# Forming the right factors of a Strassen-like down projection on VectorE instead of GpSimd, one pair of units ahead

## The chip, the cores and the metric

The kernel runs on one core of a Trainium2 chip. The metric is the device time of one execution in microseconds, the median over several runs. Engines are named as the profile names them: PE is TensorE (PEld its weight loads), DVE is VectorE, ACT is ScalarE, POOL is GpSimd, SP is SyncE, whose queue issues nearly all DMAs.

## The reference

One layer of a decoder for a prompt of 1024 tokens and 64 sample tokens (8 sequences of 8), in float32. The change lies in the two SwiGLU blocks, so only their part is shown; between them stands a mixer (windowed attention beside a gated linear recurrence) that the change does not touch.

```python
D_MODEL = 1024; D_FF = 2816; SEQ = 1024; DEC_BATCH = DEC_SEQ = 8

def swiglu(x, w_gu, w_down):
    g, u = jnp.split(x @ w_gu, 2, axis=-1)
    return (jax.nn.silu(g) * u) @ w_down

x = x + 0.5 * rms_norm(swiglu(rms_norm(x, norm_ffn1_pre), ffn1_w_gu, ffn1_w_down), norm_ffn1_post)
x = x + mixer(x)                       # attention and recurrence
x = x + 0.5 * rms_norm(swiglu(rms_norm(x, norm_ffn2_pre), ffn2_w_gu, ffn2_w_down), norm_ffn2_post)
```

## The kernel before, in words

**Tokens and precision.** The 1088 rows are cut into three groups: group 0 (320 columns, with the sample tokens), and groups 1 and 2 (384 each). Every matrix operand is split into a high and a low half (`split`, L257: ScalarE casts at L258, VectorE subtracts at L259), and a product is three matmuls (`mm3`, L279 to L281).

**Up stage.** Groups 1 and 2 are multiplied together by a seven-product scheme of the Strassen kind (products named 1 to 7) instead of eight. A unit is one tile of 128 hidden columns of gate and up weight. There are 22 units, numbered u = 0 to 21, in an order in which two successive ones (2j and 2j+1) hold hidden tiles k and k+11: that is a pair, named by its odd number. `up` (L862) walks a list of steps. A step of kind "p" is one product of 12 matmuls: `product` issues it, `evict` takes the partial result out of PSUM (L763 to L776, on ScalarE and VectorE, with a GpSimd multiplication at L760). A step of kind "c" is a piece of the same hidden tile for group 0, where that has not been done before; in the first SwiGLU the first ten units have such steps. After each step `prepare` forms and splits the right factors needed up to four steps later: the raw weights come by L709, their differences are VectorE subtractions at L722, and the splits follow. `left` (L783) combines the outputs of a pair on GpSimd (L785 to L789) and stores them to a scratch tensor FA.

**Right factors of the down projection.** The down projection uses the same seven products, with the rows k and k+11 of the down weight as blocks. Four of its right factors are sums and differences of the blocks, formed per pair during the up stage and stored to a scratch tensor FB, from which the down stage reads them much later. `right_load` (L795) loads the rows of a pair into two tiles a and b (four DMAs of 256 KB at L800, on SP). `right_form` (L803) makes four subtractions of 128x512, L806, L807, L810 and L811, and stores the results (L809, L813). In the first SwiGLU two of the four are moreover split (`in_place`, L815) and the high half stored by L820. The tiles a and b come from a pool of 12 tiles named big, out of which come also six split factors that live through the stage and one output tile per unit.

**Order.** What stands here is the order in which instructions are written. When the program is built, a planner gives every engine an order of its own from estimated costs, readiness and free tiles; an instruction can so run well ahead of its written place on its engine, but each engine's and each DMA queue's order is then fixed, and an instruction that waits holds up those behind it. At the last unit of the first SwiGLU a hook (`begin_down`) starts the loads for the down projection of group 0: weights through L265, activations through L894.

In the version before, at product 1 of unit u the pair d is loaded and after product 7 of the same unit it is formed, with d as follows:

```python
d = 1 if u == 2 else u if u % 2 and u > 1 else 0
```

Of the kernel before, what the change touches and what calls it, by code (L numbers as in the profile page):

```python
# [14 lines left out]
ALU = mybir.AluOpType  # L15
# [30 lines left out]
def tile_step(ctx: ExitStack, tc: tile.TileContext, A: dict, O: list):  # L46
    nc = tc.nc
    V, S, G, PE = nc.vector, nc.scalar, nc.gpsimd, nc.tensor
# [51 lines left out]
    def tick():  # L100
        for name in list(streams):
            st = streams[name]
            st[2] += st[1]
            while st[2] >= 1.0:
                st[2] -= 1.0
                if next(st[0], "end") == "end":
                    del streams[name]
                    break
# [540 lines left out]
    def make_ffn(wgu, wdn, h, tag):  # L649
# [93 lines left out]
        def product(u, m):  # L743
            c, first, last = CHAIN[m]
            if first:
                chains[u, c] = mmbank()
            bk = chains[u, c][:, :384]
            w, (hi, lo) = right[u, m], f.SF[m]
            for k in range(4):
                mm3(bk, (w[:, 0, k], w[:, 1, k]), (hi[:, k], lo[:, k]), first and k == 0, last and k == 3, True)  # L750

        def evict(u, m):
            j = f.units[u][0]
            if m == 1:
                outs[u] = big()
            e = outs[u]
            bk = chains[u, CHAIN[m][0]][:, :384]

            def act(i):
                G.tensor_tensor(e[:, i], e[:, i], e[:, i + 1], op=ALU.mult)  # L760

            if m == 1:
                S.copy(e[:, 0], bk)  # L763
            elif m == 2:
                V.tensor_tensor(e[:, 0], bk, e[:, 0], op=ALU.add)
                S.activation(e[:, 0], e[:, 0], AF.Silu)
            elif m == 6:
                S.copy(e[:, 1], bk)
            elif m == 7:
                S.copy(e[:, 3], bk)  # L770
                V.tensor_tensor(e[:, 3], chains[u, "Y"][:, :384], e[:, 3], op=ALU.add)
            elif m == 4:
                S.activation(e[:, 2], bk, AF.Silu)  # L773
                act(2)
            elif m == 3:
                V.tensor_tensor(e[:, 1], bk, e[:, 1], op=ALU.add)  # L776
                act(0)
                if u % 2:
                    left(u)
# [15 lines left out]
        def right_load(u):  # L795
            k = f.units[u - 1][0]
            t1, t2_ = [big(F32, (P, 3, 512)) for _ in range(2)]
            for t, kk, o in ((t1, k, 0), (t2_, k + NK, 1)):
                for half in range(2):
                    nc.sync.dma_start(t[:, half ^ o], wrow(kk, half))  # L800
            downs[u] = t1, t2_

        def right_form(u):  # L803
            k = f.units[u - 1][0]
            a, b = downs.pop(u)
            G.tensor_tensor(a[:, 2], a[:, 1], a[:, 0], op=ALU.subtract)  # L806
            G.tensor_tensor(a[:, 1], b[:, 0], a[:, 1], op=ALU.subtract)  # L807
            in_place(7, k, a[:, 1])
            nc.sync.dma_start(FB[:, k, 0:2], a[:, 1:3])  # L809
            G.tensor_tensor(b[:, 2], b[:, 0], a[:, 2], op=ALU.subtract)  # L810
            G.tensor_tensor(b[:, 1], b[:, 1], b[:, 2], op=ALU.subtract)  # L811
            in_place(4, k, b[:, 1])
            nc.sync.dma_start(FB[:, k, 2:4], b[:, 1:3])  # L813

        def in_place(m, k, t):  # L815

            if m in halves:
                hi = pp.tile([P, 512], F32R, tag="t2", bufs=8, name=uid("fh"))
                split(hi, t.bitcast(F32R), t)
                nc.sync.dma_start(FH[:, k, halves[m]], hi.bitcast(F32))  # L820

        def piece(u, i):
            w = WIDTH[0]
            if i % 2 == 0:
                chains[u, "c", i // 2] = axbank("c0")
            bk = chains[u, "c", i // 2][:, :w]
            wt = right[u, (1, 2, 8, 3)[i]]
            for k in range(4):
                mm3(bk, (wt[:, 0, k], wt[:, 1, k]), hcol(h[0], 4 * (i % 2) + k, w), i % 2 == 0 and k == 0,
                    i % 2 == 1 and k == 3)  # L830
            if i == 1:
                chains[u, "g"] = gated0(f.units[u][0], bk)
            if i == 3:
                chains[u, "g"](bk)
# [22 lines left out]
        def prepare(i):  # L857
            while f.todo and f.todo[0][0] <= i + AHEAD:
                _, u, m = f.todo.pop(0)
                factor(u, m)  # L860

        def up(hooks={}):  # L862
            for i, (kind, u, m) in enumerate(f.steps):
                if kind == "p" and m == 1 and u in hooks:
                    hooks[u]()
                if kind == "p":
                    d = 1 if u == 2 else u if u % 2 and u > 1 else 0
                    if m == 1 and d:
                        right_load(d)
                    product(u, m)  # L870
                    evict(u, m)
                    if m == 7 and d:
                        right_form(d)
                else:
                    piece(u, m)
                prepare(i + 1)
                tick()
            for d in (raws, sums, right, chains, outs):
                d.clear()
# [149 lines left out]
        f.head = head  # L1029
        f.raw0 = raw0  # L1030
        f.loads0, f.up0, f.begin, f.up, f.begin_down, f.down = loads0, up0, begin, up, begin_down, down
        f.begin_pair, f.pair, f.gated0 = begin_pair, pair, both0
        return f
# [710 lines left out]
```

## Time and profile before

| | |
|---|---|
| median of 3 runs | 2006.42 us (2005.93 to 2008.47) |
| profiled execution, own time | 2007.32 us |
| its span, first to last instruction | 2005.5 us |
| granted TensorE clock | 0.999 |
| busy share PE, DVE, ACT, POOL | 99%, 71%, 47%, 28% |
| DMA, mean over the span | 185 GB/s |
| first up stage, about | 112 to 505 us |
| second up stage, about | 1434 to 1760 us |

The page's parts are read like this: busy time by engine, the span in slices, the DMA queues, the chain of work that ended last, and the costliest groups of instructions. A group's row gives line, engine, operation, tiles written and read, shape and count, then busy microseconds, mean nanoseconds of one, the idle time of the engine just before them, and what ended it. A row of waits gives who waited for whom, total microseconds, number of times and the longest.

### The profile page before, as it was taken

Reading aid. Unit: us, or ns where it says so; the run is one execution under the profiler, and the core shown is the slowest. Engines: PE = TensorE matmul, PEld = TensorE weight load, DVE = VectorE, ACT = ScalarE, POOL = GpSimd, SP = SyncE. Lnnn points to the kernel's source line nnn. Section 1 sums busy time; section 2 is a strip of 40 time slices with the busy share of each in tenths; the row PEclk is TensorE's granted clock in tenths of the full one; section 3 lists DMA queues with packets and bytes.
Section 4 is the critical chain, followed back from the end, with each engine's and each line's share of the span. In section 5 each row is a group of like instructions: output and inputs, shape, how many; then the busy total and the mean of one; then the engine's idle time right before and its main releaser. Section 6 shows DMA issues by size and latency. Waiting matters only on the chain.

```text
span 2005.5 us, 34728 instructions
## 1 busy us (share of the span) xinstructions
PE 1982.5 (99%) x13331; PEld 1854.6 (92%) x13331; DVE 1425.8 (71%) x2321; ACT 935.4 (47%) x1697; POOL 555.7 (28%) x516
## 2 busy tenths in 40 slices
PE   9999999999999999999999999999999999999998
PEld 8999999999998987897899898989999999999886
DVE  7676767887558656777668756857888888655666
ACT  5744333444445434445344544645544444444452
POOL 2013433655104101211112311220155565510201
PEclk9999999999999999999999999999999999999999
DMA  7735446566766756766434343527566555567874
GB/s 222 229 104 177 129 156 201 196 219 232 233 220 215 189 151 219 256 166 182 135 96 138 87 141 106 175 89 236 156 200 206 188 190 191 208 231 233 286 260 138
DMA packets 377319, 370.31 MB, mean 185 GB/s; under 512 B 40546, under 2 KB 294321, under 8 KB 377137
## 3 DMA queue, kind: packets, MB, share of 16 engines
q1 hardware_dynamic: 371169, 357.21, 56.3%
q10 hardware_dynamic: 5984, 10.88, 1.6%
q8 instruction: 105, 1.72, 0.3%
q14 instruction: 61, 0.50, 0.1%
HBM read 284.31 MB, written 84.71 MB: 184 GB/s over the span
## 4 chain that ended last, share of the span: by engine, by line
PE 87%; DVE 5%; DMA 4%; issue 2%; ACT 1%; POOL 1%; SPq 0%; DVEq 0%; ACTq 0%; POOLq 0%
PE mm L279 25%; PE mm L281 25%; PE mm L280 25%; DMA raw<-in_ffn_w_gu_dram 2%; PE pv L1212 1%; PE c L281 1%; PE c L279 1%; PE c L280 1%; PE sc L1171 1%; DMA ar<-act 1%; DVE t L722 1%; DVE w L259 1%; PE pT L1199 1%; PE lv L1244 1%; DVE big L259 1%
## 5 line engine op out<-in xcount | busy, mean ns | idle before, releaser
L279 PE MATMUL mm<-h,wsph 128*128 128x320 f32 (+1 forms) x1280 | 407.9, 320 | 1.1 <-ACT sg L675 1.1
L280 PE MATMUL mm<-h,wsph 128*128 128x320 f32 (+1 forms) x1280 | 405.4, 317 | 1.9 <-POOL h L259 1.9
L281 PE MATMUL mm<-h,wspl 128*128 128x320 f32 (+1 forms) x1280 | 404.2, 317 | 2.0 <-DVE wspl L259 2.0
L259 DVE TENSOR_TENSOR wspl<-raw,wsph 128x1024 fp32r<-128x1024 f32 x200 | 251.2, 1259 | 125.4 <-ACT wsph L258 124.7
L258 ACT CAST wsph<-raw 128x1024 fp32r<-128x1024 f32 x200 | 209.2, 1049 | 275.8 <-PE mm L280 198.9
L259 DVE TENSOR_TENSOR w<-raw,w 128x512 fp32r<-128x512 f32 (+1 forms) x218 | 228.9, 1054 | 82.6 <-ACT w L258 81.2
L258 ACT CAST w<-raw 128x512 fp32r<-128x512 f32 (+1 forms) x218 | 160.3, 739 | 213.1 <-PE mm L280 112.5
L281 PEld LDWEIGHTS mm<-h,wspl 128*128 128x128 f32 x1280 | 240.0, 188 | 5.7 <-issue 2.6
L279 PEld LDWEIGHTS mm<-h,wsph 128*128 128x128 f32 x1280 | 240.2, 188 | 5.3 <-issue 2.5
L280 PEld LDWEIGHTS mm<-h,wsph 128*128 128x128 f32 x1280 | 240.4, 188 | 4.2 <-POOL h L259 2.4
L279 PE MATMUL mm<-h,w 128*128 128x384 f32 (+1 forms) x720 | 240.3, 335 | 3.0 <-DVE big L776 1.5
L280 PE MATMUL mm<-h,w 128*128 128x384 f32 (+1 forms) x720 | 240.5, 334 | 0.0
L281 PE MATMUL mm<-h,w 128*128 128x384 f32 (+1 forms) x720 | 235.1, 334 | 0.0
L279 PE MATMUL mm<-w,h 128*128 128x512 f32 x462 | 181.0, 395 | 0.2 <-DVE big L971 0.2
L280 PE MATMUL mm<-w,h 128*128 128x512 f32 x462 | 181.1, 392 | 0.0
L760 POOL TENSOR_TENSOR big<-big 128x384 f32<-128x384 f32 x88 | 112.2, 1276 | 247.5 <-ACT big L773 144.6
L281 PE MATMUL mm<-w,h 128*128 128x512 f32 x462 | 179.7, 391 | 0.0
L279 PE MATMUL mm<-big,w 128*128 128x384 f32 x528 | 176.8, 335 | 2.7 <-ACT big L763 1.3
L280 PE MATMUL mm<-big,w 128*128 128x384 f32 x528 | 176.6, 334 | 0.0
L281 PE MATMUL mm<-big,w 128*128 128x384 f32 x528 | 176.4, 334 | 0.0
L259 DVE TENSOR_TENSOR w<-t,w 128x512 fp32r<-128x512 f32 x176 | 163.2, 935 | 14.6 <-ACT w L258 14.3
L279 PEld LDWEIGHTS mm<-h,w 128*128 128x128 f32 x720 | 135.0, 188 | 4.0 <-DVE big L776 1.8
(361 smaller groups left out, 3881.8 us busy)
## 6 DMA issues: line engine op xcount, KB each, us to landing
raw<-in_ffn_w_gu_dram SPq DMA_DIRECT2D x156, 512.0 KB
raw<-in_ffn_w_down_dram SPq DMA_DIRECT2D x74, 512.0 KB
raw<-in_w_in_dram SPq DMA_DIRECT2D x54, 512.0 KB
ar<-fa SPq DMA_DIRECT2D x70, 384.0 KB
big<-in_ffn_w_down_dram SPq DMA_DIRECT2D x88, 256.0 KB
fb<-big SPq DMA_DIRECT2D x44, 512.0 KB
fa<-big SPq DMA_DIRECT2D x22, 768.0 KB
raw<-fb SPq DMA_DIRECT2D x30, 512.0 KB
```

The lines of the kernel that those rows point to most:

```text
L258: S.copy(hi, src)
L259: (lo_eng or V).tensor_tensor(lo, src, hi.bitcast(F32), op=ALU.subtract)
L279: PE.matmul(out, a[0], b[0], start=first, stop=False, skip_group_check=resume)
L280: PE.matmul(out, a[0], b[1], start=False, stop=False, skip_group_check=resume)
L281: PE.matmul(out, a[1], b[0], start=False, stop=last, skip_group_check=resume)
L722: V.tensor_tensor(t, x, y, op=ALU.subtract)
L760: G.tensor_tensor(e[:, i], e[:, i], e[:, i + 1], op=ALU.mult)
L1171: PE.matmul(banks[g][:, i * 256:i * 256 + wk], zq[64 * g:64 * g + 64, 2 * pr + i, b * P:(b + 1) * P], kx[64 * g:64 * g + 64, k0:k0 + wk], ...
L1199: PE.transpose(bank[:, (i * nk + kb) * P:(i * nk + kb + 1) * P], pt[g][:, i, kb * P:(kb + 1) * P], ident)
L1212: PE.matmul(ob[:, hd * 64:hd * 64 + 64], pT[g][:, (i * nk + kb) * P:(i * nk + kb + 1) * P], vn[:, vb, g * 64:g * 64 + 64], start=kb == 0, ...
L1244: PE.matmul(b5[cs, n_, a], x[:, a, cs], y[:, a, cs], start=True, stop=True)
```

## The change

The four subtractions of `right_form` are issued on VectorE instead of GpSimd. The unit at which a pair is loaded and formed is changed too: pair 1 stays at unit 2 and pair 3 at unit 3, pair 5 moves from unit 5 to unit 4, and from unit 5 on each odd unit loads and forms the pair two units later, so that pair 7 is done at unit 5 and pair 21 at unit 19, and unit 21 does none. The number of loads, subtractions, splits and stores is the same.

```diff
         def right_form(u):
             k = f.units[u - 1][0]
             a, b = downs.pop(u)
-            G.tensor_tensor(a[:, 2], a[:, 1], a[:, 0], op=ALU.subtract)
-            G.tensor_tensor(a[:, 1], b[:, 0], a[:, 1], op=ALU.subtract)
+            V.tensor_tensor(a[:, 2], a[:, 1], a[:, 0], op=ALU.subtract)
+            V.tensor_tensor(a[:, 1], b[:, 0], a[:, 1], op=ALU.subtract)
             in_place(7, k, a[:, 1])
             nc.sync.dma_start(FB[:, k, 0:2], a[:, 1:3])
-            G.tensor_tensor(b[:, 2], b[:, 0], a[:, 2], op=ALU.subtract)
-            G.tensor_tensor(b[:, 1], b[:, 1], b[:, 2], op=ALU.subtract)
+            V.tensor_tensor(b[:, 2], b[:, 0], a[:, 2], op=ALU.subtract)
+            V.tensor_tensor(b[:, 1], b[:, 1], b[:, 2], op=ALU.subtract)
             in_place(4, k, b[:, 1])
             nc.sync.dma_start(FB[:, k, 2:4], b[:, 1:3])
@@ up
                 if kind == "p":
-                    d = 1 if u == 2 else u if u % 2 and u > 1 else 0
+                    d = {2: 1, 3: 3, 4: 5}.get(u, u + 2 if u % 2 and 4 < u < 20 else 0)
                     if m == 1 and d:
                         right_load(d)
                     product(u, m)
```

## The prediction

> **What bounds the kernel now.** I read the head of the page first, then TensorE's waits, then the stretches of the two stages that the change touches, then VectorE's groups there.
>
> ```profile
> span 2005.5 us, 34728 instructions
> PE 1982.5 (99%) x13331; PEld 1854.6 (92%) x13331; DVE 1425.8 (71%) x2321; ACT 935.4 (47%) x1697; POOL 555.7 (28%) x516
> ```
>
> TensorE (PE) is busy for 1982.5 of 2005.5 us. GpSimd (POOL), from which work is taken, is busy for 28% and cannot be the bound as such. What can be won is idle time of TensorE, 23 us in the whole span; what can be lost is time in which TensorE is made to wait. TensorE's waits, over the whole span:
>
> ```profile
> PE mm L281 <- DVE wspl L259: 2.0, 2, 1.3
> PE mm L279 <- DVE big L776: 1.5, 1, 1.5
> PE mm L279 <- ACT big L763: 1.3, 1, 1.3
> PE mm L279 <- ACT big L770: 0.8, 1, 0.8
> PE mm L279 <- ACT big L768: 0.8, 1, 0.8
> PE mm L279 <- DVE big L771: 0.7, 1, 0.7
> ```
>
> The columns are total, number of times, longest. L763, L768, L770, L771 and L776 are the evictions of the products in the up stages of the two SwiGLUs, where the changed code runs. The chain of waits (start, length, what) gives the places of four of the stops, each ended by the instruction named:
>
> ```profile
> 344.80 0.48 DVE big L771
> ...
> 350.02 0.47 ACT big L768
> ...
> 519.15 2.04 DVE wspl L259
> ...
> 1463.07 0.56 DVE big L776
> ```
>
> Two more, on L763 and L770, fall at 490 and 504 us; their rows come below. So in the up stages TensorE stood still at 345 (0.7 us), 350 (0.8), 490 (1.3) and 504 (0.8, the last unit of the first up stage) and at 1462 (1.5, the start of the second); the stop of 1.3 us at 520, for the low half of a weight, belongs to the first down stage. That is 6.4 us in all, and no more can be won here. The stages in stretches (columns: length, then busy time of PE, PEld, DVE, ACT, POOL with counts, granted clock, DMA share, GB/s):
>
> ```profile
> 112.00:345.00 233.00, 232.63 (x1411) 232.00 (x1409) 160.35 (x247) 90.82 (x174) 85.39 (x68) 1.00 0.48 155
> 345.00:490.00 145.00, 143.92 (x828) 143.61 (x829) 123.95 (x144) 62.35 (x122) 87.14 (x60) 1.00 0.63 216
> 1480.00:1740.00 260.00, 260.00 (x1502) 260.00 (x1501) 216.76 (x247) 108.69 (x210) 151.35 (x109) 1.00 0.58 195
> ```
>
> From 1480 to 1740 us TensorE does not pause once. VectorE (DVE) is the next engine: 216.76/260 = 83% there, 85% from 345 to 490. It is where the four subtractions go, so it decides.
>
> **The change part by part.** Per pair of units GpSimd loses four subtractions of 128x512 and VectorE gains them; there are 11 pairs in each SwiGLU, 88 subtractions in all.
>
> *The work moved.* GpSimd's four rows, for nine pairs, and VectorE's rows of the same size:
>
> ```profile
> L811 POOL TENSOR_TENSOR big<-big 128x512 f32<-128x512 f32 x9 | 15.7, 1741 | 0.0
> L810 POOL TENSOR_TENSOR big<-big,big 128x512 f32<-128x512 f32 x9 | 15.3, 1699 | 0.0
> L807 POOL TENSOR_TENSOR big<-big,big 128x512 f32<-128x512 f32 x9 | 13.9, 1546 | 3.0 <-DMA big<-in_ffn_w_down_dram 2.5
> L806 POOL TENSOR_TENSOR big<-big 128x512 f32<-128x512 f32 x9 | 13.1, 1453 | 37.5 <-DMA big<-in_ffn_w_down_dram 37.5
> ...
> L259 DVE TENSOR_TENSOR w<-t,w 128x512 fp32r<-128x512 f32 x72 | 70.0, 973 | 4.9 <-ACT w L258 4.9
> L259 DVE TENSOR_TENSOR w<-raw,w 128x512 fp32r<-128x512 f32 x50 | 57.1, 1142 | 0.6
> L722 DVE TENSOR_TENSOR t<-raw,t 128x512 f32<-128x512 f32 x34 | 36.4, 1070 | 0.6
> L722 DVE TENSOR_TENSOR t<-raw 128x512 f32<-128x512 f32 x17 | 18.6, 1092 | 0.6
> L722 DVE TENSOR_TENSOR t<-raw,raw 128x512 f32<-128x512 f32 x17 | 12.8, 753 | 16.3 <-DMA raw<-in_ffn_w_gu_dram 16.3
> ...
> L722 DVE TENSOR_TENSOR t<-raw,t x88: 673/691/1776, 115.9 to 1717.7; 128x512 f32<-128x512 f32 x88
> ```
>
> The last row, minimum/median/maximum in ns, is the key: an undisturbed VectorE subtraction takes 0.69 us, but many take up to 1.78. Four more cost 4 x 0.69 = 2.8 us of VectorE per pair. What comes back: VectorE's 190 instructions of this size in the stretch took 194.9 us where 190 x 0.69 = 131 would do, an excess of 64 us. POOL's four groups hold 13.1 + 13.9 + 15.3 + 15.7 = 58.0 of its 151.35 busy us there, so their share of the excess is 0.383 x 64 = 24 us, 2.7 us for each of nine pairs. That puts all excess down to GpSimd's activity; the bounds are nothing back and the whole excess, 64/9 = 7.1 us per pair, and I take 2.7, the share by busy time, because GpSimd's other instructions stay. VectorE's load thus hardly changes: +2.8 - 2.7.
>
> The Trainium skill ("SBUF — State Buffer", section "SBUF: two separate sides") says that VectorE with two SBUF inputs and GpSimd share one port pair as an exclusive lock, held for a whole instruction, and the loser blocks fully. The row that reaches 1.78 us agrees that one holds up the other, but at full blocking by four GpSimd instructions of at least 1.45 us VectorE would win back 5.8 us per pair, 3.0 net, where the excess shows 2.7 back; TensorE would still set the time, and only the first rival below would lose ground, whose deciding wait would rise by about 3 us.
>
> *Does VectorE have the room?* A pair lasts 29.1 us, and 29.1 x (1 - 0.834) = 4.8 us of it VectorE is idle in the second SwiGLU, 29.1 x (1 - 0.855) = 4.2 us in the first. The 29.1 us is the spacing of these rows, once per pair:
>
> ```profile
> 1558.59 1.46 POOL L785 TENSOR_TENSOR big<-big,big 128x384 f32<-128x384 f32 x1
> ...
> 1587.70 1.46 POOL L785 TENSOR_TENSOR big<-big,big 128x384 f32<-128x384 f32 x1
> ```
>
> So the cover holds; if it went, each us beyond it would cost one us per pair.
>
> *The wait added.* VectorE's first subtraction of a pair now waits for the rows of the down weight. Behind it in VectorE's queue stand the differences of L722, the low halves of the weight splits of L259 that TensorE needs, and the evictions L765, L771 and L776, which free PSUM banks; ScalarE's (ACT) L766 waits for L765. How long? Two rows of the same stretch are the bounds:
>
> ```profile
> POOL big L806 <- DMA big<-in_ffn_w_down_dram: 37.5, 9, 4.8
> ...
> DVE t L722 <- DMA raw<-in_ffn_w_gu_dram: 16.3, 16, 4.9
> ```
>
> GpSimd waited 4.2 us per pair (37.5/9), having nothing else to do; VectorE waits 1.0 us per unit (16.3/16) for transfers of the same queue. Nothing is the lower end; a gain is excluded, since VectorE did not wait for these rows before. I take 1.0, for the same engine under the same load, and 1.0 fits in 4.2.
>
> *The step ahead.* From unit 5 on, load and forming of a pair sit one pair earlier in the order; units 3, 4 and 5 each hold one, and the last pair hands over nothing: its forming moves from unit 21 to 19. With it move the four loads (L800), the stores L809 and L813 and, in the first SwiGLU, two splits with their stores L820, all past the raw loads of L709 on SP's queue. In mid stage this is the same set of instructions per 29.1 us, at the same place in a unit. GpSimd already ran ahead of its written place:
>
> ```profile
> L806 POOL TENSOR_TENSOR big<-big x22: 1283/1367/2255, 134.4 to 1727.2; 128x512 f32<-128x512 f32 x22
> ...
> L763 ACT COPY big<-mm x44: 472/479/482, 111.9 to 1740.7; 128x384 f32<-128x384 f32 x44
> ```
>
> The last forming began at 1727.2 us, before even the first product of its unit was evicted (1740.7), though it is written after the last. So the step ahead is worth nothing in the middle. At the end of the first up stage it is worth something:
>
> ```profile
> 483.84 0.62 ACT L258 CAST fh<-big 128x512 fp32r<-128x512 f32 x1 [2.78 <-POOL big L811]
> ...
> 484.87 0.42 SPq L820
> ...
> 485.38 4.91 DMA ar<-act
> ...
> 491.27 0.48 ACT big L763
> ...
> 504.17 0.72 ACT L258 CAST h<-ar 128x640 fp32r<-128x640 f32 x1 [1.44 <-DMA ar<-act]
> 504.80 0.47 ACT L770 COPY big<-mm 128x384 f32<-128x384 f32 x1
> ```
>
> The first and the last two rows are ScalarE's timeline, the others the chain of waits. ScalarE waits 2.78 us for the last forming, SP's queue holds the store L820 behind that, and behind it the load of the activations for the down stage; the transfer takes 4.9 us, its cast waits for it on ScalarE, and the eviction L763 stands behind the cast, so TensorE stops for 1.3 us. With the last pair formed at unit 19 the head of this chain is gone: the load can go 2.8 us earlier, more than the 1.3 needed. The next stop, 0.8 us at 504 (L770 behind a cast that waited 1.44 us for a later one of these loads), hangs on the same queue; I take it as gone too, with bounds of 0 and 0.8. Late next is the split at 520, whose chain has the final left combinations on GpSimd in it, which stay.
>
> *What stays.* The stops at 345 and 350 us are VectorE late by GpSimd's stretch, and VectorE gets as much work as it gets relief. The stop at 1462 lies where pairs 1 and 3 keep their place. I cost these at nothing, between -3.0 (all three gone) and +3.0 (each doubled).
>
> **Sum.** The profiled execution took 2007.32 us (span 2005.5 and 1.8 around it): 2007.32 - 1.3 - 0.8 = 2005.2. The median of the runs, 2006.42, is 0.9 lower, so I predict 2004.3 us.
>
> **The rivals.** *VectorE held up by late down weights (slower).* Of VectorE's idle 4.2 to 4.8 us per pair, about 1.8 are its own waits for raw weights (16.3 us in nine pairs), which stay; 2.7 are free. From a wait of 2.7 us per pair on, VectorE becomes the bound, and the rest goes to TensorE in some 15 steady pairs (ten in the second SwiGLU, five in the first). At 3.5 us, halfway to GpSimd's 4.2, that is 0.8 x 15 = 12 us: 2018 us. For it: in the row above GpSimd waited for these loads in all nine pairs. Against it: VectorE works down a longer queue and comes to them later. Chance 0.22.
>
> *All stops go (faster).* If VectorE is in effect relieved, the six stops vanish: 2006.4 - 6.4 = 2000.0 us. For it: three of them end with VectorE late. Against it: VectorE's sum is even, and the stop at 520 has other causes. Chance 0.15.
>
> *Nothing moves.* The order in which the program is built already ran the forming ahead, and another load of the same queue takes the place of the late one at 490: 2006.4. Chance 0.15.
>
> *Crowding at units 3 to 5.* Three units in a row then form a pair; VectorE's need there is (216.76/260 x 29.1 - 2.7)/2 + 2.8 = 13.6 of 14.55 us per unit. Should two more stops of the size of that at 1462 follow, it is 2004.3 + 3.0 = 2007.3. Chance 0.10.
>
> **How the numbers follow.** The forecast has 0.38. A measurement of this kernel tells about 0.2%, 4.0 us, from no change. Forecast, nothing and crowding lie within it: 0.63 the same; faster 0.15; slower 0.22. The likeliest case's own range is 2001.3 to 2007.3 (the three stops that stay, 3.0 either way). For 8 in 10 I go from 2000.5, which leaves out half of the faster case, up to 2013, which takes in the lower half of the slower one.
>
> **What would show it.** Right: no TensorE wait on L763 near 490; VectorE's mean for 128x512 nearer 0.85 than 1.05 us; its busy share in the second up stage within 2 points of 83%; no ScalarE wait on a POOL instruction for the fh cast; TensorE unbroken from 1480 to 1740. Wrong: VectorE idle for big<-in_ffn_w_down by over 2.7 us per pair, with TensorE waits on weight splits or L771 and L776 spread over the units; or the stop at 490 still there behind another load; or a time that moves by over 4 us with the up stages unchanged in length, from an order that was laid out otherwise elsewhere.

## The result, and the profile after

The changed kernel takes 1999.36 us (median of 6 runs, 1998.05 to 2002.7), the kernel before, run beside it, 2006.63 us (6 runs, 2004.81 to 2009.83). The ratio is 0.9965, 95% interval 0.9954 to 0.9975: faster by 7.3 us, where 2.1 were predicted, and just below the predicted range of 2000.5 to 2013. The profiled execution took 2000.92 us. Head of its page:

```profile
span 1999.2 us, 34712 instructions
...
PE 1981.9 (99%) x13331; PEld 1856.7 (93%) x13331; DVE 1416.2 (71%) x2409; ACT 937.8 (47%) x1697; POOL 423.6 (21%) x428
```

TensorE is as busy as before (1981.9 us against 1982.5); its idle time fell from 2005.5 - 1982.5 = 23.0 us to 17.3. TensorE's waits, first rows of the changed kernel that matter here (who for whom: total, times, longest):

```profile
PE tr L511 <- DVE big L493: 1.9, 1, 1.9
PE mm L281 <- DVE wspl L259: 1.7, 3, 1.3
...
PE mm L279 <- ACT big L770: 0.7, 1, 0.7
```

The first, at 65 us, lies ahead of the changed code and is missing in a second profile of the same kernel (run e0 below). So does the longest of the second row (1.3, before 60 us); its other two, 0.2 each, lie near 518 and 1766 us. The last row is the only stop of the up stages, at 1448 us. Of the six stops on which the prediction was built, four are gone, that at 520 is down to 0.2, and in place of the 1.5 us at 1462 stands the one at 1448, which ends with another eviction. The stretches, with the columns of the prediction:

```profile
345.00:490.00 145.00, 145.00 (x839) 145.00 (x838) 115.18 (x158) 65.43 (x126) 65.00 (x43) 1.00 0.61 209
1480.00:1740.00 260.00, 260.00 (x1502) 260.00 (x1502) 206.72 (x279) 111.38 (x215) 88.06 (x73) 1.00 0.57 195
```

VectorE has 36 more instructions to form nine pairs from 1480 to 1740 us, and still its busy time falls from 216.76 to 206.72 us. Its groups of this size there:

```profile
L259 DVE TENSOR_TENSOR w<-t,w 128x512 fp32r<-128x512 f32 x71 | 58.2, 821 | 2.4 <-ACT w L258 2.4
L259 DVE TENSOR_TENSOR w<-raw,w 128x512 fp32r<-128x512 f32 x48 | 38.7, 807 | 4.5 <-ACT w L258 4.0
L722 DVE TENSOR_TENSOR t<-raw,t 128x512 f32<-128x512 f32 x33 | 28.2, 854 | 0.6
L722 DVE TENSOR_TENSOR t<-raw,raw 128x512 f32<-128x512 f32 x16 | 12.8, 800 | 17.7 <-DMA raw<-in_ffn_w_gu_dram 17.7
L807 DVE TENSOR_TENSOR big<-big,big 128x512 f32<-128x512 f32 x9 | 11.9, 1320 | 0.6 <-DMA big<-in_ffn_w_down_dram 0.6
L810 DVE TENSOR_TENSOR big<-big,big 128x512 f32<-128x512 f32 x9 | 11.9, 1317 | 0.0
L722 DVE TENSOR_TENSOR t<-raw 128x512 f32<-128x512 f32 x16 | 11.1, 692 | 0.5
...
L811 DVE TENSOR_TENSOR big<-big 128x512 f32<-128x512 f32 x9 | 6.9, 771 | 0.0
L806 DVE TENSOR_TENSOR big<-big 128x512 f32<-128x512 f32 x9 | 6.9, 770 | 1.6 <-issue 1.0 <-DMA big<-in_ffn_w_down_dram 0.6
```

The splits' means drop from 0.97 and 1.14 us to 0.82 and 0.81. Two of the four new subtractions take 1.32 us, not 0.69; the reason is in the section on what the runs showed of the hardware.

### The profile page after: what moved, and what is told of

The parts are those of the page before. It is cut to its first block, busy times and chain, and to the rows that moved or that the text cites. A ratio compares the mean times of both kernels' runs of the same rounds, so it can differ in the third digit from the quotient of the medians.

```text
span 1999.2 us, 34712 instructions
## 1 busy us (share of the span) xinstructions
PE 1981.9 (99%) x13331; PEld 1856.7 (93%) x13331; DVE 1416.2 (71%) x2409; ACT 937.8 (47%) x1697; POOL 423.6 (21%) x428
## 4 chain that ended last, share of the span: by engine, by line
PE 93%; DMA 3%; DVE 2%; ACT 1%; issue 1%; SPq 0%; POOL 0%; DVEq 0%; ACTq 0%
PE mm L279 27%; PE mm L281 27%; PE mm L280 27%; PE pv L1212 1%; PE c L281 1%; PE c L279 1%; PE c L280 1%; PE sc L1171 1%; DMA raw<-in_ffn_w_gu_dram 1%; DMA ar<-act 1%; PE pT L1199 1%; PE tr L511 1%; PE lv L1244 1%; DMA ar<-fa 1%; DVE wspl L259 0%
## 5 line engine op out<-in xcount | busy, mean ns | idle before, releaser
L259 DVE TENSOR_TENSOR w<-raw,w 128x512 fp32r<-128x512 f32 (+1 forms) x218 | 202.7, 934 | 83.8 <-ACT w L258 82.4
L760 POOL TENSOR_TENSOR big<-big 128x384 f32<-128x384 f32 x88 | 121.3, 1378 | 638.2 <-ACT big L773 447.7
L259 DVE TENSOR_TENSOR w<-t,w 128x512 fp32r<-128x512 f32 x176 | 137.1, 788 | 10.3 <-ACT w L258 10.3
```

The lines of the kernel that those rows point to most:

```text
L259: (lo_eng or V).tensor_tensor(lo, src, hi.bitcast(F32), op=ALU.subtract)
```

## The experiments

The theories: *relief* (R: VectorE, no longer held up by GpSimd, serves TensorE sooner), *step ahead* (A: the last pair leaves the end of the stage), *another order elsewhere* (O: the planner lays out other instructions differently), *waiting* (W: casts, low halves and stores wait for GpSimd's slow results) and VectorE's *room*. All times are medians of 5 to 11 executions, each with its ratio to the kernel before in the same rounds and the 95% interval. e0 to e3 ran on one chip, e4 to e7, e8 to e10 and e11 with e12 on three others, so across these groups the ratios are compared, not the times.

**e0: the change once more.**

> The change itself once more, beside the others on one chip: 1999.4 us, ratio 0.9965 to before. Its profile is to show whether the extra stop of 1.9 us at 65 us (a transposition that waits for VectorE's L493), which its first profile has and that of before has not, belongs to the change or to the single execution: all theories expect that it comes and goes, since no pair is formed before 130 us.

1999.0 us, ratio 0.9958 (0.9946 to 0.9971): the gain is no accident of one run. Between 340 and 520 us a single TensorE wait, of 0.2 us, is left. At the start of the second up stage there is again one on L770, of 0.8 us.

**e1: the engine alone**, the old units.

```diff
-            G.tensor_tensor(a[:, 2], a[:, 1], a[:, 0], op=ALU.subtract)
+            V.tensor_tensor(a[:, 2], a[:, 1], a[:, 0], op=ALU.subtract)
 ... (the same for the other three)
```

> The four subtractions on VectorE, but every pair loaded and formed where it was before. Theory R (relief: VectorE is held up less, and the stops of TensorE that end with a late VectorE go): the stops at 345, 350 and 1463 us go, 3.0 us, and so does what a slow last forming costs at 490 to 521; VectorE's busy time in the second up stage falls by some 10 us per 260 as with the whole change; time 2000 to 2003 us against 2006.6 before. Theory A (ahead: what is gained comes from the last pair no longer formed at the end of the stage): the stops at 490 and 504 stay, and the time is 2005 to 2007. Theory O (the planner's other order elsewhere, in the mixer, brings some 2 us of it): a gain of up to 2 us may be missing or be larger, in stages in which no pair is formed.

2000.96 us, 0.9966 (0.9952 to 0.9979): most of the gain. The stops at 490 and 504 us are gone though the last pair is formed at unit 21 as before. One stop of 1.6 us remains near 350 (TensorE's waits), as long as the two at 345 and 350 were together, so at this place the engine alone wins nothing:

```profile
PE mm L279 <- ACT big L768: 1.6, 1, 1.6
```

**e2: the step ahead alone**, on GpSimd.

```diff
-                    d = 1 if u == 2 else u if u % 2 and u > 1 else 0
+                    d = {2: 1, 3: 3, 4: 5}.get(u, u + 2 if u % 2 and 4 < u < 20 else 0)
```

> The new units for load and forming, but the four subtractions on GpSimd as before. Theory R: GpSimd still holds VectorE up, the stops at 345, 350 and 1463 stay, only the end of the first up stage gains: 2003 to 2005. Theory A: the stops at 490, 504 and 521 go, 3.4 us, and most of the gain is there: 2000 to 2003. Theory O: as in the run of the engine alone, up to 2 us either way outside the up stages.

2005.19 us, 0.9989 (0.9981 to 0.9998). The end of the first up stage is clean here too (490, 504 and 521, stops of 3.4 us in the prediction's rows), but 345 and 350 stay and a new stop of 1.7 us comes at 1510, where units 3 to 5 each form a pair. The chain of waits that ends in it (start, length, what):

```profile
1501.03 5.62 DMA raw<-in_ffn_w_gu_dram
...
1506.74 0.69 DVE t L722
1507.43 1.44 DVE w L259
...
1510.18 0.56 DVE big L771
```

A raw weight lands at 1506.6, its difference and low half follow on VectorE, and the eviction L771 stands behind them; TensorE waits. This is the prediction's crowding, on GpSimd, and one stop instead of two. The times of the two parts add up (6.1 us for e1 and 1.9 for e2, beside 8.1 for e0 in the same rounds), but the stops do not: either part alone removes nearly all of those 3.4 us, and each leaves a stop that the whole change has not, 1.6 us at 350 in e1 and 1.7 at 1510 in e2. The sum of the times is thus in part a coincidence.

**e3, e4, e5: what GpSimd's forming costs, taken apart.** e3 is the change without the four subtractions; e4 adds four GpSimd subtractions per pair whose results nobody reads; e5 adds ten GpSimd memsets per pair instead.

```diff
-            V.tensor_tensor(a[:, 2], a[:, 1], a[:, 0], op=ALU.subtract)   # all four; stores take a[:, 0:2], b[:, 0:2]
+            G.tensor_tensor(t[:, 2], t[:, 0], t[:, 0], op=ALU.subtract)   # e4: twice for t in (a, b)
+            G.memset(t[:, 2], 0.0)                                        # e5: five times for t in (a, b)
```

> As the change, but the four subtractions are left out on either engine; the raw rows are stored in their place, so the products of the down projection are those of other factors. All loads, splits and stores stay. Theory R: VectorE's 88 subtractions lie in its idle time, so the time is that of the change within 1.5 us, about 1999; VectorE's other instructions of 128x512 are as long as with the change (about 0.8 us mean). If instead the subtractions on VectorE still cost TensorE something, this is 2 to 5 us faster than the change. Theory O: a difference of up to 2 us by order alone.

> As the run without forming (1998.45 us), and GpSimd makes four subtractions of 128x512 per pair whose result nobody reads (into parts of the tiles that are not stored). What is left out is as in that run: the real forming. VectorE's own work is that of the run without forming, and no engine waits for GpSimd's results. Theory R (GpSimd's activity alone lengthens VectorE's instructions, and that makes TensorE stop): VectorE's busy time from 1480 to 1740 us rises from 184 by 24 (2.7 us per pair, as the prediction had it) to 35 us (3.9, as the change gave back), stops of TensorE after 340 and near 1460 us come back, and the time is 2002 to 2005. Rival W (before, it was the waiting for GpSimd's slow results, by the casts on ScalarE and the stores on SP's queue): the time stays at 1998 to 1999.5.

> As the run before it, but GpSimd does ten memsets of 128x512 per pair instead of four subtractions: about as much busy time (10 x 0.53 against 4 x 1.3 to 1.7 us), and nothing read. If VectorE is held up by GpSimd's reads of its memory ports alone, VectorE's instructions of 128x512 stay as in the run without forming and the time is 1998 to 1999.5. If any GpSimd instruction holds it up, it is as in the run with the four subtractions, 2002 to 2005.

e3 1998.45 us, 0.9958 (0.9945 to 0.997); e4 1999.29, 0.9963 (0.995 to 0.9975); e5 1998.15, 0.9959 (0.9946 to 0.9971). The stretch from 1480 to 1740 us in e3, then in e4 with its added GpSimd group, then in e5 with its own:

```profile
1480.00:1740.00 260.00, 260.00 (x1502) 260.00 (x1501) 184.40 (x241) 111.06 (x213) 85.43 (x72) 1.00 0.57 190
```

```profile
1480.00:1740.00 260.00, 260.00 (x1502) 260.00 (x1501) 212.41 (x243) 110.88 (x213) 140.21 (x109) 1.00 0.57 196
```

```profile
L808 POOL TENSOR_TENSOR big<-big 128x512 f32<-128x512 f32 x36 | 48.5, 1355 | 32.7 <-DMA big<-in_ffn_w_down_dram 21.5 <-issue 10.4
```

```profile
1480.00:1740.00 260.00, 260.00 (x1502) 260.00 (x1501) 183.90 (x241) 111.06 (x214) 122.69 (x150) 1.00 0.57 190
```

```profile
L808 POOL MEMSET big<- 128x512 f32 x79 | 37.4, 527 | 0.6 <-DMA fb<-big 0.6
```

Three readings. The hold-up is real: with 48.5 us of GpSimd subtractions VectorE's nearly equal number of instructions takes 212.41 - 184.40 = 28.0 us longer, 3.1 us per pair. It comes from what the GpSimd instruction does, not from GpSimd being busy: 37.4 us of memsets cost VectorE nothing (183.90). And over a whole stretch it is nearly free in the time: e4 is 1.1 us slower than e5 on the same chip, by the ratios not told apart, and VectorE's 212 us out of 260 leaves TensorE unbroken. So VectorE's busy time by itself is not where the 7 us come from; e4's VectorE is nearly as busy as that of the kernel before, and the gain is still there. One reservation: e4's subtractions need less of the pair's rows and run in other moments. Ahead of the stop at 345 they end at 333.8 us, those of the kernel before at 336.3, so e4 doesn't repeat the hold-up at that place in full. At the same units real forming on GpSimd (e2) costs 2005.19 - 1998.45 = 6.7 us, on VectorE (e0) 0.6.

**e11, e12: waiting without hold-up.** The missing corner: GpSimd memsets write the tiles that are split and stored, so that the others wait for a GpSimd chain that doesn't hold VectorE up. e11 has the new units, e12 the old ones.

```diff
-            V.tensor_tensor(a[:, 2], ...) and the other three (e12: G.tensor_tensor)
+            for i in (1, 2, 1, 2, 1, 2):
+                G.memset(a[:, i], 0.0)        # then split and store as before; the same for b
```

> The change, its units kept, but the four subtractions of a pair are replaced by GpSimd memsets of 128x512 that write the tiles which are then split and stored, three over each, so that ScalarE's casts, VectorE's low halves and SP's stores wait for a GpSimd chain of about 6.3 us per pair (12 x 0.527) as they do when GpSimd forms (four times 1.36 to 1.74). The computation left out: the right factors are zeros. A memset does not hold VectorE up, so this is the corner that is missing: waiting without hold-up, beside hold-up without waiting (0.8 us dearer than neither), neither, and both (6.7 us dearer, the version with only the units moved). Theory of the waiting: the cost of forming on GpSimd is that its results come late and the casts and stores queue behind it: 2002 to 2005, with stops at 345 to 350 and near 1510. Rival, that it takes the hold-up and the waiting together: 1998 to 2000, no more than neither alone, VectorE near 184 us busy from 1480 to 1740.

> The same memsets in the kernel before, its units kept: waiting for a GpSimd chain without VectorE being held up, and the last pair formed at unit 21. The computation left out: the right factors are zeros. Theory of the waiting: the stops at the end of the first up stage (490, 504 and 520 us, 3.9 us) are there, for they hang on the chain GpSimd, cast, store, load of the activations, and those at 345 and 350 too: 2004 to 2007. Rival, hold-up and waiting together: the stops at 490 to 520 stay at half or less, those at 345 to 350 go: 1999 to 2002.

e11 1999.9 us, 0.9969 (0.9958 to 0.998); e12 1999.86, 0.9969 (0.9958 to 0.9979). The theory of the waiting by itself falls: both land in the rival's range, and in e12 no TensorE wait of over 0.2 us is left between 340 and 520 us, with the last pair at unit 21. The four corners, new units, in ratios: neither 0.9958 (e3), hold-up alone 0.9963 (e4), waiting alone 0.9969 (e11), both 0.9989 (e2). Against e3 that is 1.0 us for hold-up alone, 2.2 for waiting alone and 6.2 for both, each to about 3 us, so that both together cost more than the sum is likely but not clear of noise. TensorE's stops in and just behind the two up stages, from 340 us on, point the same way: 0.4 us in e3, 1.2 in e4, 1.2 in e11 and 4.0 in e2. How the two can strengthen each other can be read in GpSimd's timeline of the last pair, first the kernel before, then e12 (start, length):

```profile
475.47 1.30 POOL L806 TENSOR_TENSOR big<-big 128x512 f32<-128x512 f32 x1 [5.49 <-issue]
476.84 2.15 POOL L807 TENSOR_TENSOR big<-big,big 128x512 f32<-128x512 f32 x1
...
480.65 1.46 POOL L760 TENSOR_TENSOR big<-big 128x384 f32<-128x384 f32 x1
482.07 1.74 POOL L811 TENSOR_TENSOR big<-big 128x512 f32<-128x512 f32 x1
```

```profile
470.55 0.53 POOL L807 MEMSET big<- 128x512 f32 x1 [1.87 <-DMA big<-in_ffn_w_down_dram]
...
475.54 0.53 POOL L811 MEMSET big<- 128x512 f32 x1
```

Before, the chain begins at 475.5 and ends at 483.8, each step drawn out and an L760 in between; in e12 it ends at 476.1. By this reading hold-up makes the results late and VectorE late in using them. One reservation: a memset needs fewer of the pair's loads than a subtraction, so e12's chain also begins 5 us sooner; e11 and e12 bound waiting on a short chain, and waiting on a long chain without hold-up was not tried.

**e6: VectorE's room.** The change with four more VectorE subtractions per pair.

```diff
+            for t in (a, b):
+                for _ in range(2):
+                    V.tensor_tensor(t[:, 0], t[:, 0], t[:, 0], op=ALU.subtract)
```

> The change, and VectorE makes four more subtractions of 128x512 per pair, behind the real ones, on parts of the tiles that are no longer needed: eight instead of four. Theory R with room left: VectorE's busy time from 1480 to 1740 us rises from 207 by 9 x 2.8 = 25 to 232 to 240 of 260 us, still under the bound, and the time is within 2 us of the change, 1999 to 2001. If VectorE had no room, TensorE would stop in every pair: 28 us at most and over 2005.

2009.18 us, 1.0015 (1.0006 to 1.0024): the gain is lost and more, and neither expectation was met. Stretches of the columns above, and TensorE's longest wait:

```profile
345.00:490.00 145.00, 140.27 (x804) 139.00 (x803) 123.34 (x173) 61.91 (x120) 67.88 (x42) 1.00 0.63 207
1480.00:1740.00 260.00, 257.63 (x1482) 256.45 (x1481) 231.10 (x319) 106.40 (x208) 105.68 (x72) 1.00 0.57 193
```

```profile
PE mm L279 <- ACT big L768: 6.1, 4, 3.2
```

At 231 of 260 us (89%) TensorE loses 2.4 us in nine pairs, nearly all of it before 1520 us, where three units in a row form a pair, and 4.7 between 345 and 490. The room ends at such places first, not in the steady stretch. The added subtractions also stand ahead of the pair's last split and store, so e6 makes these late as well as VectorE busy.

**e7: `left` on VectorE too.** L785 to L789 moved as well.

```diff
-            G.tensor_tensor(e[:, 1], e[:, 2], e2[:, 2], op=ALU.add)
+            V.tensor_tensor(e[:, 1], e[:, 2], e2[:, 2], op=ALU.add)
 ... (the same for the other three)
```

> The change, and the four left combinations per pair (L785 to L789, 128x384) on VectorE too. Theory R: VectorE gains 4 x 0.55 = 2.2 us per pair and loses the time that these four hold it up, which the excess in the second up stage puts at 2.2 us per pair, so its sum is even; TensorE's stops in the up stages are already gone but for about 1 us, so it is the change within 1 us, 1998 to 2000. If it is faster by over 2 us, the relief acts elsewhere than in the stops; if slower by over 2, VectorE's order is too tight for the evictions.

1998.58 us, 0.9959 (0.9946 to 0.9971): the same as the change. Its VectorE is busy for 205.52 us from 1480 to 1740, 36 shorter subtractions more and 1.2 us less than the change:

```profile
1480.00:1740.00 260.00, 260.00 (x1502) 260.00 (x1501) 205.52 (x313) 110.35 (x212) 40.90 (x36) 1.00 0.57 192
```

**e8, e9, e10: a fourth tile for raw weights.** They test a loop: VectorE late, a raw tile free late, the next raw load issued late, the next evictions late. A fourth raw tile has room only if big gives one up; e10 is that control.

```diff
-NRAW = 3
+NRAW = 4                 # e8 on the kernel before, e9 on the change; not e10
-tag="big", bufs=12
+tag="big", bufs=11       # all three
```

> The kernel before (GpSimd forms, old units) with four tiles raw for weights on their way in instead of three, and to make room eleven tiles big instead of twelve. Engine and order of the forming are untouched. Theory of the loop: GpSimd's subtractions hold VectorE up, and that costs time only where a late VectorE frees a tile raw late, so that the next raw weights are issued and land late and the evictions behind them are late too. With a fourth tile the load is issued sooner, and the stops of the kernel before at 345, 350 and 1463 us go (3.0 us) with VectorE's busy time from 1480 to 1740 still near 217 us; those at 490 to 521 us stay: 2004, and stops of the weight splits elsewhere may change too. Rival, hold-up itself: VectorE has not enough time for splits and evictions together at these places, whatever the number of tiles: 345, 350 and 1463 stay, 2007. If a tile big less hurts, the control with eleven shows it.

> The change with four tiles raw and eleven tiles big. Theory of the loop: the change has little left of these stops (0.7 us at 1448), so a fourth tile brings at most 1 us: 1998 to 1999.5. Rival, that the change left half of the loop in place, hidden in places without a stop over 0.2 us: over 2 us faster, 1997 or less.

> Control: the kernel before with eleven tiles big and three raw. The pairs' down weights and six split factors share these tiles. Theory: a free tile more or less shifts the loads of down weights by at most one unit and nothing waits for them: 2007, within 2 us of the kernel before, with the stops at 345, 350 and 1463. Rival: the loads come later, GpSimd's forming too, and the end of the first up stage is worse: 2009 or more.

e8 2019.0 us, 1.006 (1.0048 to 1.0073); e9 2011.43, 1.002 (1.0011 to 1.0029); e10 2017.17, 1.0047 (1.0033 to 1.006). The control missed: a big tile less costs 10 us, in the mixer and not in the up stages (below), so these times say little and the stretches must do. The stretch from 335 to 360 us in the kernel before, with the load L709 of SP's timeline that matters there; the stretch in e10; and both again in e8:

```profile
335.00:360.00 25.00, 23.55 (x134) 22.91 (x133) 22.24 (x30) 10.09 (x21) 11.42 (x9) 1.00 0.70 236
```

```profile
341.38 0.38 SPq L709 DMA_DIRECT2D raw<-in_ffn_w_gu_dram  x1
```

```profile
335.00:360.00 25.00, 23.67 (x135) 22.88 (x134) 22.01 (x30) 10.22 (x22) 10.23 (x8) 1.00 0.72 244
```

```profile
335.00:360.00 25.00, 25.00 (x147) 25.00 (x146) 22.71 (x28) 12.12 (x25) 12.99 (x10) 1.00 0.68 234
```

```profile
338.05 1.80 SPq L709 DMA_DIRECT2D raw<-in_ffn_w_gu_dram  x2
```

With the fourth tile the loads go out at 338 instead of 341.4 and the stops at 345 and 350 vanish, with VectorE no less busy than before. That half of the theory stands: the two stops are a matter of when the raw tile comes free. (In e0 the same load goes at 337.7, with three tiles.) The other half fails: at the start of the second up stage TensorE stops for 2.5 us in e8, more than the 1.5 of the kernel before, and e8 has a new stop of 1.1 us on L763 between 240 and 280 us.

## Why the prediction was wrong, by its own steps

**Bounds and the ceiling.** Reading TensorE's idle time as all there is to win was right in kind: the span fell by 6.3 us in the first profile and TensorE's idle time by 5.7. That the six stops are all that can be won was slightly short: the prediction's row for the low halves of down weights (wspl) holds a second stop of 0.6 us, near 1772, and in e0 both of that row are down to 0.2.

**The work moved, "+2.8 - 2.7".** The sign of the net was off, the size little. VectorE's four subtractions cost (11.9 + 11.9 + 6.9 + 6.9)/9 = 4.2 us per pair, not 2.8, since two of them are held up by GpSimd. What comes back is larger as well: the other 184 instructions of this size took 149.0 us, an excess of 22 over 0.69 each, where the 190 before had 64. Allowing for the number (64 x 184/190 = 62), that is 40/9 = 4.4 us per pair. e4 against e3 gives 3.1 for four subtractions alone. Net, about -0.2 us per pair instead of +0.1; of the 10 us by which busy time fell, about half is that six instructions fewer lie inside the stretch. The full-lock estimate of 5.8 us, set beside 2.7, is not reached by 3.1 to 4.4. The Trainium skill ("SBUF — State Buffer", section "SBUF: two separate sides") has the lock of a VectorE instruction with two SBUF inputs only against a GpSimd operation that reads SBUF; e5's memsets, which cost VectorE nothing, agree.

**The wait added, 1.0 us per pair.** Too high. VectorE's waits from 1480 to 1740 us, nine pairs:

```profile
DVE big L806 <- DMA big<-in_ffn_w_down_dram: 0.6, 1, 0.6
DVE big L807 <- DMA big<-in_ffn_w_down_dram: 0.6, 2, 0.4
```

That is 0.13 us per pair. The rival of late down weights, with a chance of 0.22 and the upper end of the range, did not come about; its 2018 us added the 12 us to the time before and left out the forecast's own gain of 2.1. The argument against it, that VectorE comes later down a longer queue, was right and got too little weight.

**The step ahead.** Right that 490 and 504 go. Wrong that the stop at 520 stays, which e0, e1 and e2 all shrink to 0.5 us or less: its chain holds another load of the activations, the same kind of transfer as the two before it (chain of waits of the kernel before):

```profile
510.32 3.85 DMA ar<-act
...
514.47 0.57 DVE big L259
...
516.03 2.86 DVE big L259 x2
```

The prediction put this stop down to GpSimd's left combinations, but from 505 to 521 us the chain holds no GpSimd instruction. That is 1.1 us, 1.3 less the 0.2 left. The prediction gave the end of the stage to the step ahead alone; e2 shows that this is enough, but e1 shows that the engine alone does it as well.

**What stays, "I cost these at nothing".** This is the step that failed, with 2.3 us: 345 and 350 are gone (0.7 + 0.8), and in place of the 1.5 at 1462 stands one of 0.7. The reasoning was that VectorE gets as much work as relief, so its lateness stays. But a sum over a stretch doesn't say when VectorE is late. Just ahead of the stop at 345 the relief is large. VectorE's timeline there, before and then in e0 (start, length):

```profile
332.42 1.03 DVE L722 TENSOR_TENSOR t<-raw,raw 128x512 f32<-128x512 f32 x1 [0.67 <-DMA raw<-in_ffn_w_gu_dram]
...
344.73 0.54 DVE L771 TENSOR_TENSOR big<-mm,big 128x384 f32<-128x384 f32 x1
```

```profile
332.90 0.68 DVE L722 TENSOR_TENSOR t<-raw,raw 128x512 f32<-128x512 f32 x1
...
339.98 0.55 DVE L771 TENSOR_TENSOR big<-mm,big 128x384 f32<-128x384 f32 x1
```

Between the two rows stand the same ten instructions, in e0 one of the new subtractions besides, and the stretch takes 12.3 us before (12.3 in e2, 10.3 in e4, 9.8 in e12) and 7.1 in e0. What counts for TensorE is when the raw tile then comes free. The load L709 in question starts at 341.4 us before; counted from the stage's first eviction L763 (at 111.9 us) that is 229.5 us. By the same count it starts at 229.3 us in e2, at 227.6 in e1, at 226.8 in e4, at 225.0 to 225.8 in the change, e0, e3, e5, e7, e11 and e12, and at 234.2 in e6. TensorE's stops around 345 and 350 us follow it: 1.5 us before, 1.3 in e2, 1.6 in e1, 0.5 in e4, none in the seven, 3.2 in e6. In e1 no GpSimd subtraction of a pair makes it late: its chain of waits holds a raw weight that took 6.8 us to land, 5.4 before. The sums do not order these runs so: e4 comes within 5 us of the old sum (212.41 of 216.76), and so does e8 (211.75), which has neither stop. The prediction's -3.0, all three gone, was near the truth and entered only as a bound. Prediction and result differ by 4.9 us: 2.3 here, 1.1 at 520, 0.4 at 1772, and about 1 more, for which see what stays open.

**Crowding at units 3 to 5.** Real on GpSimd (e2, 1.7 us), absent on VectorE: the change has no stop from 1480 to 1740 us.

**What was to be seen.** Met: no wait on L763 near 490; means near 0.85 us; TensorE unbroken from 1480 to 1740. Missed: VectorE's share is 206.72/260 = 79.5%, over 3 points below 83. Met in the letter only: ScalarE waits no longer for POOL with the fh cast, but for VectorE, shorter than before (ScalarE's waits of the changed kernel, 345 to 490 us):

```profile
ACT fh L258 <- DVE big L811: 6.9, 4, 1.7
```

**What stays open.** Of the 7.3 us, the rows of waits account for 1.5 (345 and 350), 3.2 (490 to 521), 0.8 (1462) and 0.4 (1772), 5.9 in all. They show less than the delay of TensorE's matmuls. It issues its matmuls in nearly the same order before and after (219 of 13331 differ by line and tile name, none of them in the mixer), so the starts can be compared one by one. By that, both profiles of the change gain 6.0 us from 340 to 525 us (2.0 at 345 and 350, 1.5 at 490, 1.3 at 504, 1.2 at 520), 0.7 to 0.9 at the start of the second up stage and 0.7 at 1772. The mixer, which the change does not touch, gives 0.9 us more in e0 and 2.0 in the first profile, and both come to the first up stage later than the kernel before, by 0.6 and 3.2 us. Why is open. TensorE's own order in the mixer is the same, so theory O would have to act through the other engines' order, and that this has no share isn't shown.

For the stops at 490 to 520 either part of the change is enough, and e1 and e2 show it. Those at 345 and 350 go only with both (e0): e1 and e2 keep 1.6 and 1.3 us there. That they hang on the raw load is borne out by e8 and by the series above; the rest of the chain was read from timelines. Why the start of the second up stage gains in e1, e2, e4 and e12 alike is not settled; a fourth raw tile made it worse in e8.

## What to carry to other kernels

Price a move between engines by the stops of the bounding engine, one by one, with the transfer or eviction that each hangs on, not by the balance of busy time over a stage: here 28 us of added VectorE time in nine pairs cost about 1 us, while one load issued 3.3 us late went with stops of 1.5. Work on an engine that holds another up, and whose results others then wait for, may cost more than the two effects alone: here 6.2 us beside 1.0 and 2.2, which is likely and not settled. Let a control run along when a tile count is changed: one tile less cost 10 us, in a stage that the change does not touch.

## What the runs showed of the hardware

**One instruction holds up another, both ways.** The timeline of the changed kernel while it forms one pair:

```profile
1579.38 1.01 POOL L760 TENSOR_TENSOR big<-big 128x384 f32<-128x384 f32 x1 [9.14 <-ACT big L773]
1579.46 1.48 DVE L807 TENSOR_TENSOR big<-big,big 128x512 f32<-128x512 f32 x1
...
1580.47 1.34 POOL L785 TENSOR_TENSOR big<-big,big 128x384 f32<-128x384 f32 x1
...
1580.87 1.50 DVE L810 TENSOR_TENSOR big<-big,big 128x512 f32<-128x512 f32 x1
```

Each VectorE subtraction started just after a GpSimd one and ended about 0.55 us behind its end, as if it had begun only then. In e0 it went the other way: a GpSimd L760, with a median of 1.1 us, took 5.0 while VectorE ran its instructions of 0.69 us back to back:

```profile
335.94 5.01 POOL L760 TENSOR_TENSOR big<-big 128x384 f32<-128x384 f32 x1 [7.38 <-DVE big L776]
```

**Two stops cost as much again in the clock.** In e10, whose mixer stops TensorE for 1.8 us at 1105 and 3.3 at 1110 us, the granted clock (third column from the end) falls to half for some 13 us:

```profile
1105.00:1107.00 2.00, 1.57 (x8) 0.80 (x8) 0.76 (x2) 2.00 (x10) 0.00 (x0) 1.00 0.08 23
1107.00:1110.00 3.00, 0.18 (x2) 0.00 (x0) 2.69 (x7) 0.98 (x3) 1.67 (x2) 0.59 0.00 0
1110.00:1114.00 4.00, 3.56 (x18) 3.59 (x18) 2.66 (x6) 1.65 (x4) 0.59 (x1) 0.50 0.00 0
...
1118.00:1121.00 3.00, 3.00 (x9) 2.32 (x8) 1.08 (x4) 1.49 (x1) 2.68 (x8) 0.50 0.00 0
```

The stops are five us, and e10's span (2015.2) exceeds the 2005.5 before by 9.7. A single stop of 3.2 us, in e6 at 352, left the clock at 1.00. The Trainium skill ("TensorE: Matmul & The Clock Gate", Part 1) has the clock at half after an idle window of about 3.4 us. Neither stop is that long, and only the one with another shortly before it lowered the clock; whether the idle time around a stop decides, or the small difference in length, these two runs don't show.
